# Where rows are transposed, normed and kept between the stages of a transformer block: a change to a one-core kernel

## The chip, the core and the metric

The kernel runs on one core of a Trainium2 chip. The core has a matrix engine (TensorE, "PE" in the profile, with its weight loads as "PEld"), a vector engine (VectorE, "DVE"), an activation engine (ScalarE, "ACT"), a general engine (GpSimd, "POOL") and a queue that issues most of the transfers (SyncE, "SP"). Each engine takes its instructions in the order in which the program lists them; engines wait for each other through semaphores. Data is worked on in an on-chip memory of 128 partitions (SBUF); products of PE land in eight accumulation banks (PSUM), from which DVE and ACT read. Transfers between DRAM and SBUF run on 16 DMA engines.

The metric is the time of one execution in microseconds (us) on the device.

## The reference

One transformer block on 1024 rows of 1024 features, in float32: a mixer of two sparse attentions, a cross-attention over 256 memory rows, and an MLP, each added to the residual stream. Only what the change touches is shown.

```python
def _memory_xattn(h, mem, mem_norm_g, w_xq, w_xk, w_xv, xq_norm_g, xk_norm_g, w_xo):
    m = _rms_norm(mem, mem_norm_g)
    q = _rms_norm((h @ w_xq).reshape(B, L, 4, 128), xq_norm_g)
    k = _rms_norm((m @ w_xk).reshape(B, M, 4, 128), xk_norm_g)
    v = (m @ w_xv).reshape(B, M, 4, 128)
    p = softmax(einsum('bqhd,bmhd->bhqm', q, k) * 128 ** -0.5)
    o = einsum('bhqm,bmhd->bqhd', p, v).reshape(B, L, 512)
    return o @ w_xo

def _sq_relu_mlp(h, w_ff_in, w_ff_out):
    return square(relu(h @ w_ff_in)) @ w_ff_out

x = x + _hybrid_mixer(_rms_norm(x, norm1_g), ...)      # ends in o @ w_out
x = x + _memory_xattn(_rms_norm(x, norm2_g), mem, ...)
x = x + _sq_relu_mlp(_rms_norm(x, norm3_g), w_ff_in, w_ff_out)   # 1024 -> 4096 -> 1024
```

## The kernel before

The 1024 rows are eight tiles of 128. PE needs its operands with the contracted dimension on the partitions, so rows are transposed on PE (a product with the identity `ident`) before a product uses them: `to_T` transposes up to four blocks of 128 columns into one PSUM buffer, and ACT and DVE copy the result out, either whole (one copy) or split in two parts `hi` and `lo` whose sum is the full value.

**Two streams.** The attention of the mixer (`attend`) runs over the eight tiles in order; it writes its outputs to DRAM (`oT_dr`, 64 KB pieces). Beside it runs a second stream, `fill`, which holds the rest: the projection of the later rows, `memory` (keys and values of the memory rows), then

- `between(dn, 0, 2, ...)` for tiles 0 and 1,
- `between(dn, 2, 2, ..., True)` for tiles 2 and 3,
- `mlp(dn, 0, 4, ...)`, the MLP of tiles 0 to 3,
- `between(dn, 4, 2, ...)` for tiles 4 and 5.

`together` draws from both streams by weights and paces; each `yield` hands over a weight. What attention leaves unfinished of `fill` runs after it, merged with `between(d2, 6, 2, ...)` for tiles 6 and 7, and `mlp_tail` closes with the MLP of tiles 4 to 7. On top of that order the framework orders the instructions of each engine by its own timeline before they are laid down; what is laid down is then fixed.

**`between`** does, for two tiles: load the attention output (`o_of`, eight pieces per tile, L927) and the input rows (`x2`, L931); the output product with `w_out` in four column chunks of 256, each added to `x2` (`add_to`, L918); norm and transpose (`norm_T2`); the query product with `w_xq` in two chunks; for each tile and chunk a `memory_item` (query norm, transposes, scores, softmax, transposes, values); the output product with `w_xo`, again added to `x2`.

`memory_item` writes its output `o` (128 rows by 256 columns) to DRAM at L1005 (`xo_dr`). After both chunks the rows are read back at L1011 and transposed four blocks at a time into `xh`, the buffer that had held the normed input of the query product. At the end the sums `x2` are kept in SBUF for tiles 2, 3, 6 and 7 (`keep`), and stored to DRAM (`x2_dr`, L1019) for tiles 0, 1, 4 and 5, to be loaded again by `mlp` (L1026) or `mlp_tail` (L1093).

**`norm_T2`** squares a tile with a row sum (ACT, L301), takes the inverse root (DVE L237, POOL L239), and for each half multiplies by it and by the gain (DVE, L305) and transposes (PE L282, ACT and DVE L243 and L244).

**`mlp`** norms its four tiles one after the other, then walks the 4096 features in eight groups: product with `w_ff_in`, square of the positive part, product with `w_ff_out`, added to the rows. Weights come in raw (`wraw`) and are split into `whi` and `wlo` (ACT L252, DVE or POOL L257). **`mlp_tail`** does the same for tiles 4 to 7: it loads the gain (L1086), norms tiles 4 and 5, runs two groups for them, then norms 6 and 7.

**Rings and pools.** A ring is a tag with a number of buffers; an allocation takes the one that came free first and waits until its last reader is through. In pool `dn` the tag `b4` (rows of one tile, 4 KB per partition) has four buffers. Pool `res` (tag `b4`, four buffers) lives from the end of attention to the end of the kernel; `d2` serves tiles 6 and 7; `d3`, the tail's pool, lies where `dn` was. In PSUM the tag `M` (psM) has one buffer, `D` (psD), `S` and `PT` have two.

Of the kernel before, what the change touches and what calls it, by code (L numbers as in the profile page):

```python
# [9 lines left out]
F32 = mybir.dt.float32  # L10
# [6 lines left out]
AF = mybir.ActivationFunctionType  # L17
ALU = mybir.AluOpType
# [4 lines left out]
P = 128  # L23
L = 1024
DM = 1024
# [13 lines left out]
    "p1": {"x4": 5, "st": 2, "relu": 4, "wraw": 4, "whi": 6, "wlo": 6, "c8": 4, "c4": 2, "kraw": 5, "pc": 2},  # L39
    "p2": {"x4": 5, "st": 1, "relu": 2, "whi": 4, "wlo": 4, "c8": 3, "c4": 1, "kraw": 4, "pc": 2},  # L40
    "dn": {"b4": 4, "h": 8, "relu": 2, "wraw": 2, "whi": 4, "wlo": 4},
    "res": {"b4": 4},
    "d2": {"b4": 2, "h": 8, "relu": 2, "whi": 4, "wlo": 4},
    "d3": {"g": 2, "h": 16, "relu": 2, "wraw": 4, "whi": 10, "wlo": 10},
}
PSUMS = {"p1": {"D": 4, "M": 3, "C": 1}, "main": {"S": 2, "PT": 2, "PV": 1, "D": 2, "M": 1}}
TAGS = {"p1": ("D", "M", "C"), "p2": ("D", "M", "D"), "dn": ("D", "M"), "d2": ("S", "PT"), "d3": ("D", "M")}
# [123 lines left out]
def build(nc, tc, I, C, out):  # L171
# [23 lines left out]
    def row(ap):  # L195
        return ap[None, :]
# [165 lines left out]
    KX = [[dr.tile([P, 2, 256], F32R, tag=f"KX{a}{c}", name=f"KX{a}{c}") for c in range(2)] for a in range(2)]  # L362
    VX = [[dr.tile([P, 2, 256], F32R, tag=f"VX{a}{c}", name=f"VX{a}{c}") for c in range(2)] for a in range(2)]
    x2_dr = [dr.tile([P, DM], F32, tag=f"x2{t}", name=f"x2{t}") for t in range(NT)]
    xo_dr = [dr.tile([P, 512], F32, tag=f"xo{t}", name=f"xo{t}") for t in range(NT)]


    ahead = {0: late["x"]}
# [545 lines left out]
    def residual_add(x2):  # L914
        def add_to(ci, t, pt):
            w = pt.shape[-1]
            dst = x2[t][:, ci * w:(ci + 1) * w]
            v.tensor_tensor(dst, pt, dst, op=ALU.add)  # L918
        return add_to

    def between(pool, t0, nt, x2s, keep, res=None):

        o_of = []
        for t in range(nt):
            o = ring(pool, "b4", [P, 8, P])
            for c in range(8):
                nc.sync.dma_start(o[:, c, :], oT_dr[t0 + t][c])  # L927
            o_of.append(o)
        x2 = [ring(res or pool, "b4", [P, DM]) for t in range(nt)]
        for t in range(nt):  # L930
            nc.sync.dma_start(x2[t], I["x"][0, (t0 + t) * P:(t0 + t + 1) * P, :])  # L931
        add_to = residual_add(x2)
        four = [[(c * 256, 256)] for c in range(4)]
        yield from gemm(pool, [lambda t, k: o_of[t][:, k, :]], 8, nt, W["w_out"], four, add_to)
        _, xf, xt_of = xT(pool, nt, True)

        gb2 = gain2(pool, W["norm2_g"])
        for t in range(nt):
            norm_T2(pool, x2[t], gb2, xt_of(t))
            yield 1.0  # L940

        kx, pts = [], {}

        def consume_q(ci, t, pt):
            if t == 0:
# [12 lines left out]
        def memory_item(ci, t, pt):  # L958

            (kh, kl), (vh, vl) = kx  # L960
            q = ring(pool, "relu", [P, 2, 2, P])
            p3 = pt.rearrange("p (h d) -> p h d", d=P)
            s.activation(q[:, 1], p3, AF.Square)
            ss = small(pool, "xss", 2)
            v.tensor_reduce(ss, q[:, 1], axis=AX.X, op=ALU.add)
            v.tensor_tensor(q[:, 0], p3, xqg[:, None, :].to_broadcast([P, 2, P]), op=ALU.mult)
            r = rsqrt_of(pool, ss, P, 2, "xq")
            sc = small(pool, "xsc", 4).rearrange("p (a h) -> p a h", a=2)
            v.tensor_scalar(sc[:, 0, :], r, XSCALE, None, op0=ALU.mult)
# [12 lines left out]
            v.tensor_tensor(nb, nb, sc[:, 1, :], op=ALU.mult)  # L982
            pr = ring(pool, "relu", [P, 2, 256])
            for h in range(2):
                s.activation(pr[:, h, :], sp[:, h, :], AF.Exp, bias=nb[:, h:h + 1],
                             scale=sc[:, 0, h:h + 1], accum_out=sums[:, h:h + 1])
            yield 1
            p2 = pst(TAGS[pool.name][1], [P, 2, 2, P])
            for k in range(2):
                for h in range(2):  # L990
                    te.transpose(p2[:, k, h, :], pr[:, h, k * P:(k + 1) * P], ident)
# [12 lines left out]
            v.tensor_tensor(o, pv, sums[:, :, None].to_broadcast([P, 2, P]), op=ALU.mult)  # L1004
            nc.sync.dma_start(xo_dr[t0 + t][:, ci * 256:(ci + 1) * 256], o.rearrange("p h d -> p (h d)"))  # L1005

        yield from gemm(pool, xf, 8, nt, W["w_xq"], [[(0, 256)], [(256, 256)]], consume_q)

        for t in range(nt):
            o = ring(pool, "relu", [P, 512])  # L1010
            nc.sync.dma_start(o, xo_dr[t0 + t])  # L1011
            to_T(pool, o, [x[:, 0:4] for x in xt_of(t)], 4)
            yield 0.5
        yield from gemm(pool, xf, 4, nt, W["w_xo"], four, add_to)
        for t in range(nt):
            if keep:
                x2s[t0 + t] = x2[t]
            else:
                nc.sync.dma_start(x2_dr[t0 + t], x2[t])  # L1019

    def mlp(pool, t0, nt, x2s):
        x2 = []
        for t in range(nt):
            if t0 + t not in x2s:
# [1 line left out]
                nc.sync.dma_start(x2s[t0 + t], x2_dr[t0 + t])  # L1026
            x2.append(x2s[t0 + t])
        add_to = residual_add(x2)
        (xh, xl), _, xt_of = xT(pool, nt)
        gb3 = gain2(pool, W["norm3_g"])  # L1030
        for t in range(nt):
            norm_T2(pool, x2[t], gb3, xt_of(t))
            yield 1.0

        for f4 in range(8):
# [41 lines left out]
                                          x2[t][:, c * 512:(c + 1) * 512])  # L1077
                    yield 2.6

    def mlp_tail(pool, res, x2s, t0):  # L1080

        x2 = {}
        (xh, xl), _, xt_of = xT(pool, 4)
        gb3 = [ring(pool, "g", [P, 512]) for _ in range(2)]
        for i, gb in enumerate(gb3):
            nc.sync.dma_start(gb, row(W["norm3_g"][i * 512:(i + 1) * 512]).to_broadcast([P, 512]))  # L1086

        def start(t):
            if t0 + t in x2s:
# [134 lines left out]
    dn_pool = tc.tile_pool(name="dn", bufs=1, reuse_waits="tile")  # L1224
    aw = aw_pool.__enter__()
    projected = []

    def fill():
        for part in range(1, len(PARTS)):
            with tc.tile_pool(name="p2", bufs=1, reuse_waits="tile") as p2:  # L1230
                yield from project(p2, part, late, st)
            projected.append(part)
        dn = dn_pool.__enter__()
        yield from memory(dn)
        yield 1, PACES[1]
        yield from between(dn, 0, 2, {}, False)
        yield 3, PACES[2]
        x2s = {}
        yield from between(dn, 2, 2, x2s, True)
        yield 3, PACES[3]  # L1240
        yield from mlp(dn, 0, 4, x2s)
        yield 5, PACES[4]
        yield from between(dn, 4, 2, {}, False)

    rest = fill()
    together(attend(aw, st), rest, projected)
# [1 line left out]
    sp_pool.__exit__(None, None, None)  # L1248
    at_pool.__exit__(None, None, None)
    res_pool = tc.tile_pool(name="res", bufs=1, side="right", reuse_waits="tile")  # L1250
    res = res_pool.__enter__()
    d2_pool = tc.tile_pool(name="d2", bufs=1, side="right", reuse_waits="tile")
    plan["w"] = PLAN_TAIL
    d2 = d2_pool.__enter__()
    x2s = {}
    rest = (w for w in rest if not isinstance(w, tuple))
    merge((rest, REST), (between(d2, 6, 2, x2s, True, res), 45.0))
    dn_pool.__exit__(None, None, None)
    d2_pool.__exit__(None, None, None)
    with tc.tile_pool(name="d3", bufs=1, reuse_waits="tile") as d3:  # L1260
        mlp_tail(d3, res, x2s, 4)
    res_pool.__exit__(None, None, None)
    ctx.close()

# [20 lines left out]
```

## Time and profile before

| | |
|---|---|
| median of 3 runs | 1806.75 us (1803.96 to 1807.26) |
| profiled execution: its time | 1806.83 us |
| profiled execution: span, first to last instruction | 1805.1 us |
| mean granted clock of PE | 0.979 of full speed |
| PE / DVE / ACT / POOL busy | 94% / 56% / 55% / 49% of the span |
| stores of `xo` (L1005) / reloads (L1011) | 16 of 128 KB / 8 of 256 KB |

The profile is of one execution. A row of the timeline has start, duration, engine, line, operation, out<-in by the program's names, shape and count, and in brackets the idle time of the engine just before it with what ended it. Names carry no buffer numbers. A product of float32 operands that are not split shows as two records. "PEclk" or the clock column is the clock that PE was granted. A group of lines has busy time, mean ns of one, and the idle time before with its releasers.

### The profile page before, as it was taken

How to read it: one execution, taken by the hardware profiler on the slowest of the kernel's cores; microseconds unless marked ns; L12 is line 12 of the kernel's file. 1: busy time of each engine (PE TensorE's matmuls, PEld its weight loads, DVE VectorE, ACT ScalarE, POOL GpSimd, SP SyncE). 2: the span in 40 equal slices, each digit the busy share in tenths (PEclk: the TensorE clock that was granted, in tenths of full speed). 3: DMA queues.
4: the chain of work that ended last, by engine and by line, in shares of the span. 5: the costliest groups of instructions: out<-in, count | busy, mean ns of one | idle time of the engine just before them, and what ended most of it. 6: DMA issues, size and time to landing. Idle time of an engine off the chain costs nothing.

```text
span 1805.1 us, 28037 instructions
## 1 busy us (share of the span) xinstructions
PE 1699.0 (94%) x9326; PEld 1458.2 (81%) x9326; DVE 1005.5 (56%) x2809; ACT 984.9 (55%) x2303; POOL 887.3 (49%) x1025
## 2 busy tenths in 40 slices
PE   7989999999989988999999999999999889999998
PEld 6987887788878877788878788788788778888887
DVE  4556779865885786656765667536234452222223
ACT  5444777853784688457955598555123443333333
POOL 2356557553541444575676666653111354444445
PEclk9999999899999999999999999999999899999999
DMA  7434221455336221222222121224774552333333
GB/s 199 118 129 113 64 64 58 164 161 167 97 111 188 85 61 36 60 68 71 64 75 64 63 72 60 63 70 135 229 227 124 182 155 88 95 95 96 97 120 107
DMA packets 176977, 193.80 MB, mean 107 GB/s; under 512 B 25664, under 2 KB 144192, under 8 KB 176832
## 3 DMA queue, kind: packets, MB, share of 16 engines
q1 hardware_dynamic: 168896, 181.52, 32.9%
q0 software_dynamic: 7936, 10.49, 2.1%
q8 instruction: 74, 1.21, 0.3%
q14 instruction: 71, 0.58, 0.1%
HBM read 170.98 MB, written 20.97 MB: 106 GB/s over the span
## 4 chain that ended last, share of the span: by engine, by line
PE 53%; DVE 7%; ACT 5%; issue 3%; DMA 2%; POOL 1%; SPq 0%; DVEq 0%; POOLq 0%; ACTq 0%
PE psD L224 39%; PE psS L224 7%; PE psPV L224 3%; PE psPT L721 2%; ACT dmask L662 2%; DMA relu<-xo 1%; DVE tkj L663 1%; ACT whi L252 1%; DMA whi<-in_w_out_dram 1%; PE psM L282 1%; ACT S L706 1%; ACT ph L243 1%; DVE pl L244 1%; DVE S L704 0%; POOL wlo L257 0%
## 5 line engine op out<-in xcount | busy, mean ns | idle before, releaser
L257 POOL TENSOR_TENSOR wlo<-wraw,whi 128x512 fp32r<-128x512 f32 (+1 forms) x225 | 307.8, 1373 | 272.4 <-ACT whi L252 269.6
L224 PE MATMUL psD<-whi,h 128*128 128x512 f32 x1024 | 338.4, 399 | 9.7 <-DVE b L1150 7.1
L252 ACT ACTIVATE whi<-wraw 128x512 fp32r<-128x512 f32 x321 | 200.3, 627 | 220.6 <-PE psD L224 158.4
L224 PEld LDWEIGHTS psD<-whi,h 128*128 128x128 f32 x1024 | 191.7, 189 | 53.5 <-DVE b L1150 10.9
L224 PE MATMUL psD<-xh,whi 128*128 128x512 f32 (+1 forms) x576 | 212.8, 373 | 1.6 <-ACT xh L243 1.5
L224 PE MATMUL psD<-xh,wlo 128*128 128x512 f32 (+1 forms) x576 | 213.1, 371 | 0.0
L224 PE MATMUL psD<-xl,whi 128*128 128x512 f32 (+1 forms) x576 | 211.2, 369 | 0.0
L224 PE MATMUL psD<-wlo,h 128*128 128x512 f32 x512 | 201.6, 396 | 0.3 <-POOL wlo L257 0.3
L224 PE MATMUL psD<-wlo,xh 128*128 128x256 f32 (+1 forms) x704 | 192.5, 355 | 2.9 <-DMA wlo<-in_w_in_dram 2.4
L224 PE MATMUL psD<-whi,xh 128*128 128x256 f32 (+1 forms) x704 | 191.3, 353 | 1.5 <-DVE Vd L244 0.9
L244 DVE TENSOR_TENSOR pl<-psPT,ph 128x512 fp32r<-128x512 f32 (+1 forms) x232 | 141.7, 619 | 58.9 <-ACT ph L243 58.0
L706 ACT ACTIVATE S<-S,mn 128x128 f32<-128x128 f32 (+7 forms) x192 | 142.9, 745 | 50.4 <-DVE mn L704 49.3
L243 ACT ACTIVATE ph<-psPT 128x512 fp32r<-128x512 f32 (+1 forms) x232 | 122.1, 540 | 86.2 <-PE psPT L721 76.6
L257 DVE TENSOR_TENSOR wlo<-wraw,whi 128x512 fp32r<-128x512 f32 (+1 forms) x96 | 81.5, 849 | 149.6 <-ACT whi L252 149.6
L711 POOL TENSOR_SCALAR S<-S,sums,gi 128x640 f32<-128x640 f32 (+7 forms) x128 | 105.3, 832 | 100.2 <-DVE sums L709 95.2
L224 PEld LDWEIGHTS psD<-wlo,xh 128*128 128x128 f32 x704 | 132.9, 194 | 14.1 <-DMA wlo<-in_w_in_dram 2.8
L224 PEld LDWEIGHTS psD<-whi,xh 128*128 128x128 f32 x704 | 131.3, 194 | 11.6 <-DVE Vd L244 1.1
L721 PE MATMUL psPT<-c_ident,S 128*128 128x128 f32 x816 | 133.9, 278 | 7.0 <-POOL S L711 2.1
L224 PEld LDWEIGHTS psD<-xh,whi 128*128 128x128 f32 x576 | 108.5, 188 | 19.1 <-ACT xh L243 2.0
L224 PEld LDWEIGHTS psD<-xl,whi 128*128 128x128 f32 x576 | 108.6, 189 | 17.6
L224 PEld LDWEIGHTS psD<-xh,wlo 128*128 128x128 f32 x576 | 108.5, 188 | 17.0
L224 PE MATMUL psS<-K,qh 128*128 128x384 f32 (+3 forms) x288 | 111.7, 392 | 9.9 <-DVE mn L704 6.1
(289 smaller groups left out, 3830.2 us busy)
## 6 DMA issues: line engine op xcount, KB each, us to landing
wraw<-in_w_ff_in_dram SPq DMA_DIRECT2D x40, 512.0 KB, 4.0
wraw<-in_w_ff_out_dram SPq DMA_DIRECT2D x40, 512.0 KB, 3.9
wraw<-in_w_ff_in_dram SPq DMA_DIRECT2D x64, 256.0 KB, 2.8
wraw<-in_w_ff_out_dram SPq DMA_DIRECT2D x64, 256.0 KB, 2.7
whi<-in_w_out_dram SPq DMA_DIRECT2D x32, 256.0 KB, 4.2
wlo<-in_w_out_dram SPq DMA_DIRECT2D x32, 256.0 KB, 4.1
wraw<-in_w_in_dram SPq DMA_DIRECT2D x24, 256.0 KB, 3.7
q<-st SPq DMA_DIRECT2D x12, 512.0 KB, 2.8
```

The lines of the kernel that those rows point to most:

```text
L224: te.matmul(o, a, b, start=start, stop=stop)
L243: s.activation(hi, src, AF.Copy)
L244: v.tensor_tensor(lo, src, hi, op=ALU.subtract)
L252: s.activation(hi, raw, AF.Copy)
L257: (v if l == "v" else g).tensor_tensor(lo, raw, hi, op=ALU.subtract)
L282: te.transpose(pt[:, j, :], x_t[:, (c + j) * P:(c + j + 1) * P], ident)
L662: s.activation(mask, src, AF.Sign, bias=tks[:, i, 1:2], accum_out=over[:, 0:1])
L663: v.scalar_tensor_tensor(small(aw, "tkj", 3), over, nd, tks[:, i, :], op0=ALU.is_gt, op1=ALU.mult, accum_out=tks[:, i + 1, 1:2] if b else ...
L706: s.activation(S, S, AF.Exp, bias=low, scale=-1.0, accum_out=sums[:, hh:hh + 1])
L711: g.tensor_scalar(Ss[hh], Ss[hh], sums[:, hh:hh + 1], 1.0 if gate is None else gate[:, hh:hh + 1], op0=ALU.mult, op1=ALU.mult)
L721: te.transpose(p2[:, j, hh, :], S[:, (c + j) * P:(c + j + 1) * P], ident)
```

## The change

Three things move, and two rings change with them.

1. `memory_item` no longer stores `o`. It transposes it at once (two blocks) into `xo`, a fifth row tile of tag `b4`; `xo_dr`, the stores and the reloads are gone, and the product with `w_xo` reads `xo`.
2. For tiles 2 and 3, `between` alternates its product with `w_xo` with `pre_norms`, which norms tiles 0 and 1 for the MLP: tile 0 is loaded whole, tile 1 in two halves into `wraw`. `mlp` then norms tiles 2 and 3 alone. The rows of tile 1 are loaded a second time for the residual sum.
3. For tiles 4 and 5, once `res` is open, the sums are written to tiles of `res` (`kept`) by the last add and handed to `mlp_tail` in `x2s`; they are neither stored nor loaded. The gain `gb3` moves from `d3` to `res` and is loaded as soon as `res` is open.

```diff
-    "res": {"b4": 4},
+    "res": {"b4": 4, "g": 2},
-    "d3": {"g": 2, "h": 16, "relu": 2, "wraw": 4, "whi": 10, "wlo": 10},
+    "d3": {"h": 16, "relu": 2, "wraw": 4, "whi": 10, "wlo": 10},
...
-    def between(pool, t0, nt, x2s, keep, res=None):
+    def between(pool, t0, nt, x2s, keep, res=None, then=None):
...
         kx, pts = [], {}
+        xo = ring(pool, "b4", [P, 4, nt * P])
...
             v.tensor_tensor(o, pv, sums[:, :, None].to_broadcast([P, 2, P]), op=ALU.mult)
-            nc.sync.dma_start(xo_dr[t0 + t][:, ci * 256:(ci + 1) * 256], o.rearrange("p h d -> p (h d)"))
+            yield 1
+            to_T(pool, o.rearrange("p h d -> p (h d)"), [xo[:, ci * 2:ci * 2 + 2, t * P:(t + 1) * P]], 2)
...
-        for t in range(nt):
-            o = ring(pool, "relu", [P, 512])
-            nc.sync.dma_start(o, xo_dr[t0 + t])
-            to_T(pool, o, [x[:, 0:4] for x in xt_of(t)], 4)
-            yield 0.5
-        yield from gemm(pool, xf, 4, nt, W["w_xo"], four, add_to)
+        if not keep and "res" in late:
+            kept = [ring(late["res"], "b4", [P, DM]) for t in range(nt)]
+            x2s.update((t0 + t, kept[t]) for t in range(nt))
+
+            def add_to(ci, t, pt):
+                cs = slice(ci * 256, (ci + 1) * 256)
+                v.tensor_tensor(kept[t][:, cs], pt, x2[t][:, cs], op=ALU.add)
+        last = gemm(pool, [lambda t, k: xo[:, k, t * P:(t + 1) * P]], 4, nt, W["w_xo"], four, add_to)
+        yield from alternate(last, then()) if then else last
         for t in range(nt):
             if keep:
                 x2s[t0 + t] = x2[t]
-            else:
+            elif t0 + t not in x2s:
                 nc.sync.dma_start(x2_dr[t0 + t], x2[t])
 
+    def pre_norms(pool, made, x2s):
+
+        made["x"] = xT(pool, 4)
+        made["g"] = gain2(pool, W["norm3_g"])
+        xt_of = made["x"][2]
+        x2s[0] = ring(pool, "b4", [P, DM])
+        nc.sync.dma_start(x2s[0], x2_dr[0])
+        norm_T2(pool, x2s[0], made["g"], xt_of(0))
+        yield 1.0
+        halves_ = []
+        for c in range(2):
+            halves_.append(ring(pool, "wraw", [P, 512]))
+            nc.sync.dma_start(halves_[c], x2_dr[1][:, c * 512:(c + 1) * 512])
+        xs = xt_of(1)
+        ss = [small(pool, "nss", 1) for _ in range(2)]
+        for c in range(2):
+            s.activation(xs[0][:, c * 4:c * 4 + 4], halves_[c].rearrange("p (k c) -> p k c", c=P), AF.Square, accum_out=ss[c])
+        v.tensor_tensor(ss[0], ss[0], ss[1], op=ALU.add)
+        r = rsqrt_of(pool, ss[0], DM, 1, "n")
+        yield 0.5
+        for c in range(2):
+            xn = ring(pool, "relu", [P, 512])
+            v.scalar_tensor_tensor(xn, halves_[c], r[:, 0:1], made["g"][c], op0=ALU.mult, op1=ALU.mult)
+            to_T(pool, xn, [x[:, c * 4:c * 4 + 4] for x in xs], 4)
+            yield 0.5
+
-    def mlp(pool, t0, nt, x2s):
+    def mlp(pool, t0, nt, x2s, made):
...
-        (xh, xl), _, xt_of = xT(pool, nt)
-        gb3 = gain2(pool, W["norm3_g"])
-        for t in range(nt):
-            norm_T2(pool, x2[t], gb3, xt_of(t))
+        (xh, xl), _, xt_of = made["x"]
+        for t in range(2, nt):
+            norm_T2(pool, x2[t], made["g"], xt_of(t))
             yield 1.0
...
-    def mlp_tail(pool, res, x2s, t0):
+    def mlp_tail(pool, res, x2s, t0, gb3):
...
-        gb3 = [ring(pool, "g", [P, 512]) for _ in range(2)]
-        for i, gb in enumerate(gb3):
-            nc.sync.dma_start(gb, row(W["norm3_g"][i * 512:(i + 1) * 512]).to_broadcast([P, 512]))
...
-        x2s = {}
-        yield from between(dn, 2, 2, x2s, True)
+        x2s, made = {}, {}
+        yield from between(dn, 2, 2, x2s, True, None, lambda: pre_norms(dn, made, x2s))
...
-        yield from between(dn, 4, 2, {}, False)
+        yield from between(dn, 4, 2, late["x2s"], False)
...
-    res = res_pool.__enter__()
+    res = late["res"] = res_pool.__enter__()
+    gb3 = [ring(res, "g", [P, 512]) for _ in range(2)]
+    for i, gb in enumerate(gb3):
+        nc.sync.dma_start(gb, row(W["norm3_g"][i * 512:(i + 1) * 512]).to_broadcast([P, 512]))
...
-    x2s = {}
+    x2s = late["x2s"]
...
-        mlp_tail(d3, res, x2s, 4)
+        mlp_tail(d3, res, x2s, 4, gb3)
```

More of the change, by code (lines that the diff above doesn't have):

```diff
@@ L364, in build @@
     x2_dr = [dr.tile([P, DM], F32, tag=f"x2{t}", name=f"x2{t}") for t in range(NT)]
-    xo_dr = [dr.tile([P, 512], F32, tag=f"xo{t}", name=f"xo{t}") for t in range(NT)]
     ahead = {0: late["x"]}
@@ L931, in between @@
             nc.sync.dma_start(x2[t], I["x"][0, (t0 + t) * P:(t0 + t + 1) * P, :])
-        add_to = residual_add(x2)
-        four = [[(c * 256, 256)] for c in range(4)]
+        add_to, four = residual_add(x2), [[(c * 256, 256)] for c in range(4)]
         yield from gemm(pool, [lambda t, k: o_of[t][:, k, :]], 8, nt, W["w_out"], four, add_to)
@@ L1226, in build @@
     projected = []
+    late["x2s"] = {}
     def fill():
@@ L1237, in fill @@
         yield 3, PACES[2]
-        x2s = {}
-        yield from between(dn, 2, 2, x2s, True)
+        x2s, made = {}, {}
+        yield from between(dn, 2, 2, x2s, True, None, lambda: pre_norms(dn, made, x2s))
         yield 3, PACES[3]
-        yield from mlp(dn, 0, 4, x2s)
+        yield from mlp(dn, 0, 4, x2s, made)
         yield 5, PACES[4]
-        yield from between(dn, 4, 2, {}, False)
+        yield from between(dn, 4, 2, late["x2s"], False)
     rest = fill()
```

## The prediction

> **What bounds the kernel now.** I read the page first, then the granted clock, then where TensorE (PE) stands still.
>
> ```profile
> span 1805.1 us, 28037 instructions
> PE 1699.0 (94%) x9326; PEld 1458.2 (81%) x9326; DVE 1005.5 (56%) x2809; ACT 984.9 (55%) x2303; POOL 887.3 (49%) x1025
> ...
> PE 53%; DVE 7%; ACT 5%; issue 3%; DMA 2%; POOL 1%; SPq 0%; DVEq 0%; POOLq 0%; ACTq 0%
> ```
>
> PE sets the pace: it is busy for 94% of the span and no other engine for more than 56%. The change alters no product of the big weights, so it can gain only from the 1805.1 - 1699.0 = 106.1 us in which PE is idle and from time at a halved clock. The second view cuts out the two stages that the change rearranges: the attention over the memory of tiles 2 and 3 with the start of the MLP after it (641 to 730), and the same change of stage in the tail (1382 to 1442). Its columns are busy us of the engines, granted clock, DMA share and GB/s.
>
> ```profile
> 641.00:670.00 29.00, 27.21 (x165) 24.22 (x165) 22.45 (x83) 26.53 (x59) 13.27 (x15) 1.00 0.20 56
> 670.00:699.50 29.50, 20.97 (x115) 17.25 (x116) 27.49 (x80) 25.32 (x57) 14.38 (x19) 0.88 0.06 17
> ...
> 1382.00:1397.00 15.00, 14.36 (x76) 12.47 (x74) 5.79 (x18) 2.84 (x9) 0.69 (x1) 1.00 0.35 110
> 1397.00:1401.00 4.00, 2.80 (x19) 2.25 (x19) 1.97 (x4) 2.54 (x7) 0.00 (x0) 0.98 0.82 277
> 1401.00:1418.00 17.00, 9.13 (x33) 7.26 (x34) 10.41 (x14) 7.65 (x16) 6.25 (x6) 0.50 0.83 256
> 1418.00:1442.00 24.00, 24.00 (x159) 22.49 (x158) 6.92 (x14) 9.22 (x19) 9.51 (x12) 1.00 0.41 132
> ...
> 1134.60:1138.00 3.40, 3.40 (x11) 2.63 (x10) 3.40 (x7) 2.23 (x5) 3.32 (x3) 0.50 0.27 83
> 1264.30:1267.70 3.40, 3.40 (x9) 2.69 (x10) 0.00 (x0) 0.00 (x0) 0.96 (x2) 0.50 1.13 375
> ```
>
> From 670 to 699.5 VectorE (DVE) is full (27.49 of 29.5) and ScalarE (ACT) nearly, because four norms run there beside attention and no big product is at hand; PE idles 8.5 us, and the mean clock of 0.88 means some 7 us at 0.5, another 3.5 us lost. From 1397 to 1418 PE idles 1.2 + 7.9 us, and its 9.13 busy us at clock 0.50 are worth 4.6, so 13.6 us are lost there. PE's own rows, with the idle time before each in brackets, show who is waited for:
>
> ```profile
> 1393.15 1.03 PE L224 MATMUL psD<-whi,xh 128*128 128x256 f32 x4
> 1394.02 1.03 PE L224 MATMUL psD<-wlo,xh 128*128 128x256 f32 x4
> ...
> 1397.77 1.33 PE L224 MATMUL psS<-h 128*128 128x128 f32 x10
> 1398.94 0.51 PE L991 MATMUL psPT<-c_ident,relu 128*128 128x128 f32 x3
> ...
> 1405.98 1.11 PE L282 MATMUL psM<-c_ident,relu 128*128 128x128 f32 x4 [2.66 <-DVE relu L305]
> 1408.57 1.11 PE L282 MATMUL psM<-c_ident,relu 128*128 128x128 f32 x4 [1.47 <-DVE xl L244]
> 1410.79 1.12 PE L282 MATMUL psPT<-c_ident,relu 128*128 128x128 f32 x4 [1.11 <-DMA relu<-xo]
> 1414.53 1.09 PE L282 MATMUL psM<-c_ident,relu 128*128 128x128 f32 x4 [2.62 <-DVE xl L244]
> ...
> 1418.20 0.47 PE L224 MATMUL psD<-xh,whi 128*128 128x256 f32 x1
> ```
>
> The last output product of tiles 4 and 5 ends near 1394.9 and the first MLP product starts at 1418.2, 23.3 us later. The queues say why: first SP's issues, then one row each of DVE, ACT and GpSimd (POOL).
>
> ```profile
> 1392.88 0.34 SPq L1019 DMA_DIRECT2D x<-b  x1
> 1395.56 0.34 SPq L1093 DMA_DIRECT2D b<-x  x1
> ...
> 1399.97 0.92 SPq L1086 DMA_DIRECT2D g<-in_norm_g_dram  x2
> ...
> 1401.41 1.00 SPq L1104 DMA_DIRECT2D wraw<-in_w_ff_in_dram  x2
> ```
> ```profile
> 1405.18 0.75 DVE L305 SCALAR_TENSOR_TENSOR relu<-b,nr,g 128x512 f32<-128x512 f32 x1 [3.80 <-DMA g<-in_norm_g_dram]
> ```
> ```profile
> 1408.72 1.14 ACT L252 ACTIVATE whi<-wraw 128x512 fp32r<-128x512 f32 x2
> ```
> ```profile
> 1409.94 3.30 POOL L257 TENSOR_TENSOR wlo<-wraw,whi 128x512 fp32r<-128x512 f32 x2 [0.29 <-ACT whi L252]
> ```
>
> The sums of tile 4 go out to DRAM and come back, the gain vector is asked for only at 1399.97, and the first weights of the MLP stand behind both in SP's queue.
>
> **The change, part by part.** The order of the built instructions, compared engine by engine, tells where each part went.
>
> **Sums of 4 and 5 to the tail's room.** Two stores (x<-b) and two reloads (b<-x) go, and the gain is loaded far ahead. In the new order the transposes of norms 4 and 5 stand among the queries of tiles 6 and 7, and between the last output product of 4 and 5 and the first MLP product stand 15 query products, 18 transposes and 12 narrow products. A 256-column product takes 0.43 us (two rows, 1393.15 to 1394.02, are 0.87 apart for two products of two records each), a transpose 0.15 to 0.17, a narrow one 0.13: 6.5 + 2.9 + 1.6 = 11.0 us of work. The weights could be there sooner: their buffers come free with that last output product, and from issue to the first split were at most 1408.72 - 1401.41 = 7.3 us, plus 0.6 (ACT) and 1.65 (POOL) for the split, 9.6 us. So the wait for weights is covered, with 1.4 us to spare; if the cover is gone it costs what is over. The item chains of tiles 6 and 7 (softmax between products) now have MLP products to hide behind. What is late next is the odd softmax link (0.7 us before) and perhaps one stretch at half clock: 3.6 us left of 13.6, gain 10. Bounds: 4 (only the waits on the gain and the stores, 2.66 + 1.11, go) and 13.6.
>
> The clock term rests on idle time driving the clock, as the rows at 1134.6 and 1264.3 suggest: 3.4 us at 0.50 each. [...]
>
> **Norms of 0 and 1 beside the product of 2 and 3.** What one norm costs, from the groups of lines between 641 and 700:
>
> ```profile
> L305 DVE SCALAR_TENSOR_TENSOR relu<-b,nr,h 128x512 f32<-128x512 f32 x8 | 6.4, 806 | 1.2 <-POOL nr L239 0.7 <-PE psM L282 0.5
> ...
> L244 DVE TENSOR_TENSOR xl<-psM,xh 128x512 fp32r<-128x512 f32 x7 | 4.7, 678 | 0.3 <-ACT xh L243 0.3
> ...
> L301 ACT ACTIVATE xh<-b 128x1024 fp32r<-128x1024 f32 x4 | 4.2, 1048 | 0.0
> L243 ACT ACTIVATE xh<-psM 128x512 fp32r<-128x512 f32 x7 | 4.1, 590 | 0.4 <-PE psM L282 0.3
> ```
>
> DVE 2 x 0.806 + 2 x 0.678 = 3.0 us, ACT 1.05 + 2 x 0.59 = 2.2 us. Two norms take 6.0 us of DVE out of the stretch where DVE is the limit, which shortens it by about that, and some 1.7 us of half clock go with it. They land in 641 to 670, where DVE has 6.5 us free but ACT only 2.5 for 4.4: 1.9 us are paid there. The new order has 80 PE rows without a big product where there were 139, the rest now lies beside MLP products. Net 6.0 + 1.7 - 1.9 = 5.8; because waits in the crowded stretch can come at the wrong time I take 4. Bounds: a loss of 2 (nothing freed, ACT paid) and a gain of 9 (three quarters of 12). The two half loads of tile 1 and the gain's place in the queue add three SP issues of about 0.35 us in a stage where DMA is busy for 0.20; they are hidden by attention.
>
> **Memory rows transposed at once.** Sixteen stores and eight reloads go, and with them PE's waits on the reload outside the tail stretch. The new short transposes (two instead of four at a time) share the one buffer psM with the norms:
>
> ```profile
> PE psM L282 <- DVE xl L244: 11.2, 5, 3.8
> PE psD L224 <- DVE b L918: 3.6, 3, 2.2
> PE psM L282 <- DMA relu<-xo: 3.2, 3, 1.7
> ```
>
> The gain is 3.2. In the new order 13 or more PE rows stand between an item's value products and its transposes, so they rarely wait; I charge 1.2 and keep 2. Bounds: 0 and 3.2. **The ring** pays: five row tiles go through four buffers (tag b4). The loads of tile 3's attention output must wait until the output product of 0 and 1 has ended, and the input rows of 2 and 3 queue behind them on SP, with output weights behind those. Before:
>
> ```profile
> x<-b SPq DMA_DIRECT2D x4, 512.0 KB, 4.1
> b<-o SPq DMA_DIRECT2D x64, 64.0 KB, 2.1
> b<-in_x_dram SPq DMA_DIRECT2D x8, 512.0 KB, 4.3
> ```
>
> Nine issues of 0.46 us (the row at 1399.97 has two in 0.92) and a landing of 2.1 put tile 3 there 6.2 us after that product; the input rows of tile 2 land at 4.1 + 4.3 = 8.4, and the add that frees a product buffer takes another 0.4. PE has one tile's product (eight at 0.43, 3.5 us), ten attention instructions (at 0.17, 1.7) and the second tile's product (3.5) to do meanwhile, 8.7 us. So it is a tie, where PE now waits 2.2 us (second row of the waits above, its longest); I charge 1 more, and 5 if the store, too, is slow.
>
> **Sum.** -10 - 4 - 2 + 1 = -15 on the profiled execution: span 1805.1, its time 1806.8, so 1.7 us lie around it. 1790.1 + 1.7 = 1791.8, say **1792 us**. That execution lies 0.1 above the median of 1806.75, so nothing is corrected. All gains at their best and no loss give 1806.8 - 25.8 = 1781; all at their worst 1806.8 - 4 + 2 + 5 = 1810.
>
> **Rivals.** (1) The weights of the first MLP products are late all the same. For it: four 512 KB blocks start at once, DMA is at 0.83 there, and four loads for the product of 6 and 7 stand ahead of them on SP. Against: 7.3 us was measured in that very crowd. If the distance of 23.3 us stays, 12.3 are left over the 11.0 of cover, and PE, which goes in order, holds the items of 6 and 7 back with it; the tail gains 1.3: 1800.5. (2) The half clock does not follow from these gaps and stays: 4.6 + 1.7 us come back, 1798. Against it: clock and idle time fall together in every row above. [...] (3) Slower: the single psM buffer. Twelve short rounds and four rounds of norms 0 and 1 now come between products that PE takes in order; a waited-for round cost 11.2 / 5 = 2.2 us. At seven such waits the 15 us are gone, with ten it is 1806.8 - 15 + 22 = 1814. For it: ACT and DVE, which empty psM, are full between 641 and 700. Against it: those 11.2 us are five waits in the whole run, mostly where PE had nothing else. (4) The stall only moves: the items' own softmax chains become what PE waits for in the tail, and the crowded ACT undoes the gain at 670; tail -3, the rest 0: 1804. That the sums of 4 and 5 still pass through DRAM is no rival: the stores x<-b fall from 4 to 2 in the built order.
>
> **How the numbers follow.** Forecast 1786 to 1798: 0.52; more than that, below 1786: 0.09; rival 1: 0.13; rival 2: 0.06; rival 4: 0.09; rival 3: 0.11. What a measurement of this kernel can tell from no change is about 0.2%, 3.6 us, so faster means below 1803.1: 0.52 + 0.09 + 0.13 + 0.06 = 0.80; same, up to 1810.4: 0.09; slower 0.11. The range is 1781 to 1805: it leaves out rival 3 and half of what may lie below.
>
> **What would show it.** After: no relu<-xo among PE's waits; no stretch of ten and more us at clock 0.50 near 1400; the first xh,whi product within some 12 us of the last output product of 4 and 5; PE above 25 of 29.5 us in the stretch before the MLP's first product; the L918 wait before the second output product of 2 and 3 between 1 and 7 us. The forecast is wrong if psM L282 rises above 20 us among PE's waits, if wraw is what PE or ACT waits for in the tail, or if the half clock lasts with the idle time gone.

## The result, and the profile after

Four runs of the changed kernel have a median of 1793.9 us (1789.2 to 1796.5), four of the kernel before beside them 1806.9 us (1804.0 to 1807.3). The ratio is 0.9929, 95% interval 0.9905 to 0.9952: faster by 0.7%, near the 1792 us of the prediction. The profiled execution took 1789.2 us. Its first lines, in the form of the page of before:

```profile
span 1787.5 us, 27978 instructions
PE 1688.9 (94%) x9326; PEld 1452.9 (81%) x9326; DVE 1008.9 (56%) x2810; ACT 984.9 (55%) x2313; POOL 891.2 (50%) x1025
```

PE's idle time is 1787.5 - 1688.9 = 98.6 us, where it was 106.1, and its busy time is 10.1 us shorter with the same 9326 records, most of it time at half clock: the mean clock is 0.984, where it was 0.979. So the gain of this pair of profiles is made of waits and clock; 5.7 us of it lie ahead of the first point that the change touches, as the last section says. The same stretches as in the prediction, in the view by windows (busy us of PE, PEld, DVE, ACT and POOL, granted clock, DMA share, GB/s): the 29.3 us before the MLP's first product, then the tail, and a stretch that was not expected to matter, 1295.6 to 1302.4.

```profile
648.00:677.30 29.30, 24.86 (x142) 22.08 (x141) 24.32 (x79) 27.85 (x64) 16.53 (x21) 0.88 0.24 75
1376.00:1387.80 11.80, 7.94 (x41) 6.62 (x39) 8.05 (x14) 7.32 (x15) 7.05 (x7) 1.00 0.93 303
1387.80:1394.60 6.80, 4.54 (x19) 3.91 (x20) 6.27 (x14) 2.02 (x4) 2.66 (x3) 0.50 0.68 245
...
1295.60:1302.40 6.80, 3.42 (x8) 2.76 (x9) 0.00 (x0) 0.00 (x0) 1.69 (x4) 0.50 1.01 305
```

Before the MLP, DVE fell from 27.5 to 24.3 us and PE rose from 21.0 to 24.9; ACT is the fuller engine there now (27.85 us), and the clock is 0.88 as before. In the tail, 1376.0 to 1394.6 loses 3.9 + 2.3 us of idle time and 2.3 at half clock, 8.4 in all, where 13.6 were lost: a gain of 5.2. The last line takes it back. PE's rows with the waits in both places, first the one of before, then those of after:

```profile
1304.09 0.45 PE L224 MATMUL psS<-whi,b 128*128 128x256 f32 x1 [1.79 <-DMA whi<-in_w_out_dram]
```
```profile
1298.98 0.80 PE L224 MATMUL psS<-whi,b 128*128 128x256 f32 x1 [4.95 <-DMA whi<-in_w_out_dram]
...
1375.70 0.38 PE L224 MATMUL psD<-wlo,b 128*128 128x256 f32 x1
...
1385.58 0.50 PE L224 MATMUL psS<-h 128*128 128x256 f32 x2 [2.15 <-ACT h L243]
1389.44 0.69 PE L282 MATMUL psPT<-c_ident,relu 128*128 128x128 f32 x2 [3.36 <-DVE relu L965]
...
1395.64 0.39 PE L224 MATMUL psD<-xh,whi 128*128 128x256 f32 x1 [0.75 <-ACT xh L243]
```

The output product of tiles 6 and 7 waited 1.79 us for its weights before; now it waits 4.95, and the clock halves around it (3.42 busy us there are worth 1.7). That is 3.2 + 1.7 = 4.9 us lost against 5.2 won. The second profile of the changed kernel (after_again below) agrees: there the wait is 6.77 us, and of the 19.6 us from the last output product of 4 and 5 to the MLP's first product 6.7 are idle, here 6.9. In the tail it is no longer weights, gain or sums that PE waits for, but the items of tiles 6 and 7 themselves. SP's rows of before, and then of after, show where the 4.95 us come from, and two lines of what SP itself waited for among the pieces of after:

```profile
1290.34 0.59 SPq L735 DMA_DIRECT2D o<-oc  x1
1290.98 6.78 SPq L927 DMA_DIRECT2D b<-o  x14
1297.86 0.85 SPq L931 DMA_DIRECT2D b<-in_x_dram  x2
1298.75 0.43 SPq L273 DMA_DIRECT2D whi<-in_w_out_dram  x1
```
```profile
1281.43 0.93 SPq L1280 DMA_DIRECT2D g<-in_norm_g_dram  x2
1282.45 0.59 SPq L734 DMA_DIRECT2D o<-oc  x1
1283.09 1.07 SPq L930 DMA_DIRECT2D b<-in_x_dram  x2
...
1284.73 10.40 SPq L926 DMA_DIRECT2D b<-o  x16
1295.23 0.38 SPq L273 DMA_DIRECT2D whi<-in_w_out_dram  x1
```
```profile
SPq L926 <- DMA b<-in_x_dram: 1.6, 2, 1.0
SPq L926 <- DMA g<-in_norm_g_dram: 1.0, 2, 0.8
```

From the store of attention's last output (o<-oc) to the issue of the first output weight it was 8.4 us and is now 12.8. Gain and input rows are issued ahead of the pieces of the attention output, all sixteen pieces stand behind the store, where it was fourteen, and they take 10.4 us instead of 6.8. The pieces are not dearer to issue one by one (median 0.43 us in both): between them SP stands still until the rows and the gain that it has just issued have landed, 2.6 us in all. Before, SP had no such wait among its pieces.

### The profile page after: what moved, and what is told of

Read it like the earlier page. It is cut to its first block, busy times and chain, and to the rows that moved or that the text cites. A ratio compares the mean times of both kernels' runs of the same rounds, so it can differ in the third digit from the quotient of the medians.

```text
span 1787.5 us, 27978 instructions
## 1 busy us (share of the span) xinstructions
PE 1688.9 (94%) x9326; PEld 1452.9 (81%) x9326; DVE 1008.9 (56%) x2810; ACT 984.9 (55%) x2313; POOL 891.2 (50%) x1025
## 4 chain that ended last, share of the span: by engine, by line
PE 65%; DVE 10%; ACT 9%; DMA 5%; POOL 5%; issue 4%; SPq 1%; ACTq 0%; POOLq 0%; DVEq 0%
PE psD L224 48%; PE psS L224 8%; ACT dmask L661 4%; PE psPV L224 3%; PE psPT L720 3%; ACT S L705 2%; POOL wlo L257 1%; DVE pl L244 1%; DVE S L703 1%; PE psM L282 1%; DVE tkj L662 1%; ACT whi L252 1%; DMA wraw<-in_w_ff_in_dram 1%; ACT ph L243 1%; POOL S L710 1%
## 5 line engine op out<-in xcount | busy, mean ns | idle before, releaser
L224 PE MATMUL psD<-whi,h 128*128 128x512 f32 x1024 | 343.7, 402 | 9.4 <-DVE b L1175 5.4
L224 PE MATMUL psD<-wlo,xh 128*128 128x256 f32 (+1 forms) x608 | 165.7, 348 | 2.8 <-DMA wlo<-in_w_in_dram 2.4
L224 PE MATMUL psD<-whi,xh 128*128 128x256 f32 (+1 forms) x608 | 165.9, 347 | 1.3 <-DVE Vd L244 0.9
L224 PEld LDWEIGHTS psD<-wlo,xh 128*128 128x128 f32 x608 | 113.6, 193 | 11.4 <-DMA wlo<-in_w_in_dram 2.8
L224 PEld LDWEIGHTS psD<-whi,xh 128*128 128x128 f32 x608 | 112.9, 193 | 9.4 <-DVE Vd L244 1.1
```

Of the source, the lines that this page charges most:

```text
L224: te.matmul(o, a, b, start=start, stop=stop)
```

## The experiments

Each kernel was timed in five rounds against the kernel before on the same chip; as the times of before differ from chip to chip (medians 1807 to 1814 us), the ratio is what is compared. PE's idle time is span less busy time of the profiled execution, the clock is of that execution.

| kernel | ratio to before, 95% | PE idle us | clock |
|---|---|---|---|
| before | 1 | 106.1 | 0.979 |
| the change | 0.9929 (0.9905 to 0.9952) | 98.6 | 0.984 |
| after_again: the change once more | 0.9932 (0.9911 to 0.9953) | 104.0 | 0.980 |
| a_once: transposes at once alone | 0.9888 (0.9869 to 0.9908) | 99.5 | 0.983 |
| b_kept: sums kept, gain early, alone | 1.0012 (0.9993 to 1.0031) | 107.2 | 0.976 |
| e_norms: norms of 0 and 1 alone | 0.9973 (0.9955 to 0.9991) | 106.2 | 0.978 |
| c_no_norms: a_once and b_kept | 0.9906 (0.9887 to 0.9924) | 99.8 | 0.981 |
| a_head: at once, tiles 0 to 3 only | 0.9877 (0.9850 to 0.9905) | 94.0 | 0.980 |
| a_tail: at once, tiles 4 to 7 only | 0.9948 (0.9929 to 0.9968) | 103.4 | 0.985 |
| x_head_paced: a_head, yields left in | 0.9926 (0.9904 to 0.9949) | 98.8 | 0.979 |
| x_before_unpaced: before, yields out | 0.9933 (0.9910 to 0.9957) | 99.8 | 0.982 |
| g_late: c_no_norms, gain moved | 0.9875 (0.9851 to 0.9898) | 95.7 | 0.986 |
| x_after_late: the change, gain moved | 0.9910 (0.9886 to 0.9934) | 104.6 | 0.981 |
| g_late_split: g_late, two queues | 0.9837 (0.9813 to 0.9861) | 94.1 | 0.982 |

**The parts one by one.** On the kernel before, first the transposes alone:

```diff
-            nc.sync.dma_start(xo_dr[t0 + t][:, ci * 256:(ci + 1) * 256], o.rearrange("p h d -> p (h d)"))
+            yield 1
+            to_T(pool, o.rearrange("p h d -> p (h d)"), [xo[:, ci * 2:ci * 2 + 2, t * P:(t + 1) * P]], 2)
...
-        for t in range(nt):
-            o = ring(pool, "relu", [P, 512])
-            nc.sync.dma_start(o, xo_dr[t0 + t])
-            to_T(pool, o, [x[:, 0:4] for x in xt_of(t)], 4)
-            yield 0.5
```

> The kernel before with the memory rows transposed at once alone (fifth row tile in the ring of four buffers, no stores and reloads of xo; norms and sums as before). Theory P, the terms of the prediction: -2 for the waits on the reload, +1 for the ring, so 1806 (-1 against before). Theory S, that the gain sits in the stages and not in the terms as I cut them: on record after the change, the stretch from the last output product of 4 and 5 to the first MLP product of the tail shrank by 3.6 us only, and the transposes now stand among the queries of 6 and 7; by it most of the tail's gain comes from not waiting for the reload relu<-xo, which holds PE's order, and this part alone brings 4 to 7 us: 1800 to 1803. Either way no relu<-xo among PE's waits; the wait on the gain (relu<-b,nr,g) stays in the tail.

Measured 0.9888, some 20 us: three times the larger of the two forecasts, and more than the whole change. The wait on the gain nearly went too, from 3.3 to 1.0 us (psM L282 <- DVE relu L305), against both expectations. The edit also takes out two `yield 0.5` per call, which matters below.

The kept sums alone are the change's third part put on the kernel before: `kept`, `x2s` handed on, `gb3` in `res`.

> The kernel before with the sums of 4 and 5 kept in res and the gain loaded early, alone (xo still through DRAM, norms of 0 to 3 in the MLP). Theory P: -10, so 1797. Theory S: the items of 6 and 7 and their reload of xo are what PE then waits for between the last output product of 4 and 5 and the MLP: -3 to -6, so 1801 to 1804. Both: no wait on g in the tail; by P no stretch of ten and more us at clock 0.50 near the start of the tail, by S one of about 7 or more stays.

Measured 1.0012: nothing, or a small loss. PE's rows of that kernel and the windows of two stretches at half clock:

```profile
1311.69 0.79 PE L224 MATMUL psS<-whi,b 128*128 128x256 f32 x1 [6.13 <-DMA whi<-in_w_out_dram]
...
1408.87 0.66 PE L282 MATMUL psM<-c_ident,relu 128*128 128x128 f32 x4 [2.10 <-DVE relu L305]
1415.14 2.39 PE L224 MATMUL psS<-h 128*128 128x128 f32 x10 [1.38 <-DVE h L244]
```
```profile
1410.20:1423.90 13.70, 9.91 (x45) 9.16 (x44) 10.63 (x15) 7.56 (x15) 8.04 (x5) 0.50 0.62 194
1307.80:1314.60 6.80, 2.91 (x7) 2.38 (x8) 0.00 (x0) 0.00 (x0) 0.00 (x0) 0.50 1.07 333
```

The tail still loses 3.8 us of idle time and 5.0 at half clock in 1410.2 to 1423.9, with no gain and no sums to wait for: norms and items hold PE. And the weights of 6 and 7 come late here too, 6.13 us, which with the half clock behind that wait (2.91 busy us are worth 1.5) costs 4.3 + 1.5 us and takes back what the tail wins, 13.6 - 8.8.

The norms alone are `pre_norms` beside the w_xo product of 2 and 3.

> The kernel before with the norms of tiles 0 and 1 beside the w_xo product of 2 and 3, alone. Theory P: -4, so 1803. Theory S, by the place of the MLP's end in the trace after the change (14.7 us earlier, of which 5.7 were there before the change could act): -7 to -9, so 1798 to 1800. Both: DVE below 27 of 29.5 us in the stretch before the MLP's first product.

Measured 0.9973, 5 us: the prediction's 4 was right for this part by itself. Then the changed kernel without `pre_norms`, that is, the first and third part together:

> The changed kernel with the norms of tiles 0 and 1 back in the MLP (the two other parts stay). Theory P: -11, so 1796. Theory S: -4 to -7, so 1800 to 1803, since most of the gain is the norms'. If the parts add up, this time and that of the norms alone have differences from before that sum to that of the whole change, -13.

Measured 0.9906, some 17 us, more than either forecast. The parts don't add up: 0.9888, 1.0012 and 0.9973 multiplied give 0.9873, the whole gives 0.9929. Whether that was chance was asked with the changed kernel, unaltered:

> The changed kernel, unaltered, once more, to set it beside the parts on one chip. Theory Q (the transposes at once bring the whole gain; the two other parts give some of it back): ratio to before 0.992 to 0.994 as in the first measurement, so 4 to 9 us slower than the transposes alone (ratio 0.9888). Rival (the first measurement and that of the parts differ by chip or by luck): ratio 0.988 to 0.990, as the transposes alone.

0.9932. Its interval and that of the transposes alone, taken on two chips, don't touch (that of the first measurement, from 0.9905, just does): **the transposes bring more than the whole change, and the two other parts together give back some 0.4%.**

**Where the transposes gain.** `once = t0 < 4`, or `t0 >= 4`, chooses between the new path and the old per call of `between`.

> Transposed at once for tiles 0 to 3 only; tiles 4 to 7 go through DRAM as before, norms and sums as before. By the trace of the kernel with the transposes alone, the stages from the first output product of 2 and 3 to the end of the MLP of 0 to 3 are 12.7 us shorter, of which about 4 are attention work put off to later, and the rest up to the norms of 6 and 7 is 3.9 us shorter with these 4 in it. Theory Q1 (both places gain): about -8 here, ratio 0.995 to 0.9965. Rival Q2 (the tail gains nothing by itself, what is seen there comes from attention having moved): -14 to -18, ratio 0.990 to 0.992. Rival Q3 (all gain in the tail): ratio above 0.998.

> Transposed at once for tiles 4 to 7 only; tiles 0 to 3 through DRAM as before. Q1: about -8, ratio 0.995 to 0.9965, with no relu<-xo wait after 1300 us and the first tail product of the MLP earlier by 8 or more. Q2: ratio above 0.998. Q3: 0.989 to 0.991.

0.9877 and 0.9948: each place gains by itself, but the first alone already gives what both give. No theory said so. Built, the kernel with the tail's transposes has PE in the same order as before until 1344 us, so its 9 us are of the tail alone. (Its two calls lose their yields too, and the streams of the tail are merged by the same weights; how much of the 9 us is the reload and how much the order was not tried apart.) The windows from the psD<-h wait near 485 us to the MLP's first product, through the MLP of 0 to 3, and on to the norms of 6 and 7: all three of before, the last one of tail only, then all three of head only.

```profile
485.06:699.20 214.14, 193.68 (x1150) 168.33 (x1150) 161.61 (x538) 151.66 (x364) 80.31 (x113) 0.98 0.35 104
699.20:1253.04 553.84, 540.35 (x2806) 451.44 (x2807) 336.42 (x861) 356.03 (x714) 355.44 (x350) 0.99 0.22 68
1253.04:1476.67 223.63, 201.87 (x1129) 177.08 (x1128) 90.56 (x195) 74.88 (x160) 58.82 (x69) 0.95 0.62 191
```
```profile
1255.28:1468.75 213.47, 197.57 (x1129) 173.34 (x1128) 92.16 (x195) 75.18 (x164) 60.14 (x69) 0.99 0.60 190
```
```profile
481.81:692.95 211.14, 196.28 (x1150) 171.66 (x1150) 157.64 (x533) 151.31 (x366) 79.38 (x112) 0.94 0.32 98
692.95:1240.75 547.80, 536.22 (x2781) 449.14 (x2780) 335.17 (x853) 353.05 (x709) 355.03 (x349) 0.99 0.21 69
1240.75:1459.09 218.34, 202.79 (x1156) 179.60 (x1154) 93.96 (x209) 78.01 (x169) 61.45 (x71) 0.97 0.62 195
```

With the tail's transposes alone the last stretch is 10.2 us shorter with the same 1129 PE records: 5.9 us less idle, the rest clock (0.95 to 0.99). The MLP's first product of the tail is not earlier for it, though that was foretold (1420.96, before 1418.20); instead 110 PE records stand between it and the last output product of 4 and 5, where 64 stood. With the head's alone it is 5.3 us shorter although it holds 27 records more and its memory rows still pass through DRAM: idle time falls there from 21.8 to 15.6 us by another order alone. The MLP's 6.0 us are 4.1 of busy time, most of it attention work put off to the last stretch, and 1.9 of idle time. Ahead of the MLP idle time falls from 20.5 to 14.9 us, of which the clock of that execution (0.94) takes some back.

**Order or reload?** Those two `yield 0.5` per call count, since `together` weighs its two streams by what they yield (`df += w or 0.0`). So that was tried apart for tiles 0 to 3: the yields left in, and, in the kernel before, set to nothing for tiles 0 to 3 with the reloads left.

```diff
+            for t in range(nt):
+                yield 0.5
```

> The kernel with the transposes at once for tiles 0 to 3 only (ratio 0.9877), but with the two yields of 0.5 per call left in that stood behind the reloads; they count as work in the weights by which the second stream and attention take turns, so taking them out let the second stream run 1.0 ahead per call, and from PE's 3400th product on the instructions are interleaved otherwise. Theory reload (stores, reloads and their place in PE's order are what costs): ratio stays at 0.986 to 0.990. Rival pace (the gain is a better interleave of the MLP of 0 to 3 with attention that the two yields decide): ratio 0.995 to 1.000, of which at most 3 us are the reload's.

```diff
-            yield 0.5
+            yield 0.5 if t0 >= 4 else 0.0
```

> The kernel before, with stores and reloads of the memory rows, and the two yields of 0.5 behind the reloads of tiles 0 to 3 set to 0. Theory reload: ratio 0.998 to 1.002. Rival pace: ratio 0.988 to 0.992.

0.9926 and 0.9933: both theories fall as put, each has half. Without touching one transfer, four yields of 0.5 (two in each of two calls) are worth 0.7%; with them kept, the reloads of tiles 0 to 3, with the new places of the transposes, are worth 0.7%. With the yields kept the stretch up to the MLP's first product is 6.2 us shorter than before and its idle time falls from 20.5 to 15.1 us:

```profile
484.21:692.20 207.99, 192.88 (x1150) 168.63 (x1150) 157.42 (x533) 150.88 (x364) 79.38 (x112) 0.97 0.33 100
```

The MLP's stretch in the kernel before with the yields out, and what PE waits for between 700 and 1240 us, first of before, then of this kernel:

```profile
698.76:1244.80 546.04, 538.42 (x2793) 451.11 (x2794) 335.57 (x855) 354.09 (x711) 354.53 (x348) 0.99 0.22 69
```
```profile
PE psS L224 <- DVE mn L704: 4.5, 3, 2.1
PE psS L224 <- ACT ir L628: 3.5, 2, 2.4
...
PE psPT L721 <- DVE sums L709: 1.4, 1, 1.4
```
```profile
PE psS L224 <- ACT ir L628: 5.1, 3, 3.0
...
PE psS L224 <- DVE mn L704: 0.2, 1, 0.2
```

Idle time there falls from 13.5 us (553.84 - 540.35) to 7.6. Two waits on attention's own chain (mn, sums) are all but gone, 5.9 us before; the one on ir grows by 1.6.

**The weights of tiles 6 and 7.** The load of the gain was moved in the code behind the output product of 6 and 7, in the kernel without the early norms and in the changed one:

```diff
+        if res:
+            for i, gb in enumerate(late["gb3"]):
+                nc.sync.dma_start(gb, row(W["norm3_g"][i * 512:(i + 1) * 512]).to_broadcast([P, 512]))
         _, xf, xt_of = xT(pool, nt, True)
```

> Transposes at once and sums of 4 and 5 kept, norms of 0 and 1 back in the MLP, and the gain of the tail's norms loaded only behind the output weights of 6 and 7, not as soon as its room opens. Beside it stands the same kernel with the gain loaded first (ratio 0.9906; PE waits 7.7 us for w_out of tiles 6 and 7 there, 1.9 with the transposes alone). Theory Q (gain and rows taken ahead on SP push the pieces of the attention output and the weights back): the wait on w_out of 6 and 7 falls to 2 to 4 us and the ratio to 0.986 to 0.988. Rival R (the room's new layout delays the pieces, whatever the gain's place): the wait stays at 5 to 8 us and the ratio at 0.990 to 0.992.

> The changed kernel with one thing other: the gain of the tail's norms is loaded behind the output weights of 6 and 7. Theory Q (in the kernel without the early norms this step took the wait on w_out of 6 and 7 from 7.7 to 2.6 us and the ratio from 0.9906 to 0.9875): wait from 5 to 7 down to 2 to 3 us, ratio 0.989 to 0.991, 4 to 6 us below the changed kernel. Rival: the gain is only late elsewhere (a wait on g in the norms of 4 and 5 of 2 us and more), ratio 0.992 to 0.994.

PE's rows: without the early norms and with the gain first (c_no_norms), then with the gain moved (g_late), then the changed kernel with it moved; behind each of the last two, SP's rows.

```profile
1307.35 1.22 PE L224 MATMUL psS<-whi,b 128*128 128x256 f32 x2 [7.68 <-DMA whi<-in_w_out_dram]
```
```profile
1301.16 0.80 PE L224 MATMUL psS<-whi,b 128*128 128x256 f32 x1 [2.63 <-DMA whi<-in_w_out_dram]
...
1284.53 0.90 SPq L936 DMA_DIRECT2D g<-in_norm_g_dram  x2
1285.53 0.85 SPq L734 DMA_DIRECT2D o<-oc  x1
...
1297.45 0.38 SPq L273 DMA_DIRECT2D whi<-in_w_out_dram  x1
```
```profile
1310.22 0.80 PE L224 MATMUL psS<-whi,b 128*128 128x256 f32 x1 [7.49 <-DMA whi<-in_w_out_dram]
...
1290.75 2.04 SPq L935 DMA_DIRECT2D g<-in_norm_g_dram  x2
...
1302.69 1.14 SPq L273 DMA_DIRECT2D whi<-in_w_out_dram  x1
```

The edit didn't do what I meant. The planner put the gain ahead of the pieces all the same, only behind the input rows (in the changed kernel behind the store as well), so the time from the last store to the first output weight hardly changed (11.9 and 13.3 us, after 13.9 in c_no_norms and 12.8 in the change). In g_late the wait fell and so did the ratio, though the intervals 0.9875 and 0.9906 overlap by a hair; in the changed kernel the wait stayed and the ratio of 0.9910 can't be told from 0.9932. A gain that really comes behind the pieces was not tried. What holds is the comparison of kernels: where sums and gain sit in `res`, the wait is 4.95 and 6.77 (the change, twice), 6.13, 7.68, 7.49 and, in g_late, 2.63 us; before it is 1.79, with the transposes alone 1.87, with the norms alone 3.39.

Last, SP's burden itself: g_late with every other piece of tiles 6 and 7 on POOL's queue.

```diff
-                nc.sync.dma_start(o[:, c, :], oT_dr[t0 + t][c])
+                (g if res and c % 2 else nc.sync).dma_start(o[:, c, :], oT_dr[t0 + t][c])
```

> Transposes at once, sums kept, gain late (ratio 0.9875), and every other piece of the attention output of tiles 6 and 7 issued on POOL's queue instead of SP's. If SP's sixteen issues in a row (0.4 to 0.65 us each) are what the output weights of 6 and 7 wait for, the wait falls from 2.6 to under 1 us and the time by 2 to 3 us: ratio 0.985 to 0.987. Rival: the pieces are late for another reason (POOL's own work delays its issues, or the landing rules): ratio 0.987 to 0.990.

```profile
1288.60 0.59 SPq L734 DMA_DIRECT2D o<-oc  x1
...
1296.12 0.38 SPq L273 DMA_DIRECT2D whi<-in_w_out_dram  x1
...
1299.79 0.48 PE L224 MATMUL psS<-whi,b 128*128 128x256 f32 x1 [1.37 <-DMA whi<-in_w_out_dram]
```

From store to weight it is 7.5 us again, the wait 1.37 (not under 1), and 0.9837 the best ratio of all, 1.6% below the kernel before and below the range foretold. Against g_late, measured on another occasion, the intervals overlap (0.9851 to 0.9861), so how much of it is the second queue's stays open.

## Why the prediction was right, and where it was not

The time was right (1792 against 1793.9 us), and the sign. The sum behind it was not: its terms were -10, -4, -2 and +1, and two of them, measured alone, lie outside their bounds. That they cancelled is luck.

- **Sums kept, -10.** Bounds -4 to -13.6; alone it measures +2 us (-1 to +6). The step that failed is the attribution of the tail's 13.6 us: I read the waits on gain and sums and SP's order as their cause, and charged the cure to the sums alone. The same edit put gain and rows ahead of sixteen pieces on SP and made PE wait 4 us longer for w_out of 6 and 7, a wait that the sum doesn't have: I counted what comes sooner and not what stands behind it on the same queue. In the changed kernel the account is 5.2 won and 4.9 lost.
- **Weights covered.** Right: no wait on wraw in the tail. But the MLP's first product came 19.6 us after the last output product (1395.64 - 1376.08), not within 12, since PE waits 2.15 + 3.36 us for the items and works 4.5 us at half clock. That is rival 4's mechanism in the tail; it had a chance of 0.09, with 3 us left of the tail's gain.
- **Transposed at once, -2.** Bounds 0 and 3.2; alone it measures some -20. The step that failed is the price: the waits that name relu<-xo. Transposing at once in the tail is worth 9 us there, yields included, by idle time and clock in a stretch whose rows name other waits. In the head it is worth 13 us with the yields kept, of which 6.2 show up to the MLP's first product (214.14 to 207.99): twice the 3.2 of the named waits in that stretch alone. The other half of the 22 with the yields out is those yields, which the diff shows and I didn't price: they change how the MLP of 0 to 3 and attention alternate.
- **The ring, +1.** It cost nothing that shows: before the second output product of 2 and 3, the waits below stand in after where 2.15 us (on b, L918) stood, and the first is just within the 1 to 7 foretold.

```profile
546.93 1.13 PE L224 MATMUL psD<-whi,b 128*128 128x256 f32 x4 [1.27 <-DVE b L917]
550.73 1.13 PE L224 MATMUL psD<-wlo,b 128*128 128x256 f32 x4 [0.94 <-DMA wlo<-in_w_out_dram]
```

- **Norms, -4.** Alone -5. On top of the two other parts the ratio goes from 0.9906 to 0.9929 and 0.9932, so no gain is left and perhaps a loss; the intervals overlap. PE in the stretch before the MLP is at 24.86 of 29.3, just short of the 25 foretold, but the 1.7 us of half clock that were to go there stayed (0.88). With the MLP starting 16 us earlier (22 by the profiles, less the 5.7 won ahead of the change), its own stage became longer; which order costs there was not settled. The part also yields 2.5 in `between` where `mlp` yielded 2.0, ahead of the change of pace, and no run parts this from the norms themselves.
- **Half clock.** The 17 us stretch is gone with part of the idle time; 6.8 us remain in the first profile. In the second profile of the same kernel 10.2 us remain, from 1399.2 on, and the forecast's "no stretch of ten and more" fails there. So rival 2 holds in part: of its 4.6 us 2.3 remain in the first profile, and the 1.7 before the MLP stayed. That idle time drives the clock, by which both terms went into the sum, was my estimate from rows of before; no run shows it by itself, as the last section says. Rival 3, the single psM buffer, is out: psM's waits on xl fell from 11.2 to 5.1 us among PE's waits:

```profile
PE psM L282 <- DVE xl L244: 5.1, 3, 3.8
```

## What to carry to other kernels

A right total proves nothing of its terms: run each part alone, since here one part alone beat the whole by 0.4%. In a kernel whose order is laid by a planner, look for what an edit does to the weights that it counts: four yields of 0.5, with no instruction changed, moved the time as much as taking out the eight stores and four reloads of the head. And the loads taken ahead were paid for here by what stood behind them on their queue: from the store to the first output weight 8.4 us became 12.8, in 2.6 of which the queue stood still until those loads had landed. So find the next thing for which an engine waits there before you call it free, and see in the built queue that the load went where the code says.

## What the runs showed of the hardware

The half clock came in pieces of 3.4 us (3.40, 6.80, 13.70 in the windows above), and the same wait did not always bring it. In the 17 us at 0.50 of the kernel before, from 1401 on, PE's longest wait is 2.66 us. In the two rows from which the prediction ties the clock to idle time, 1134.6 and 1264.3, PE is busy for all of the 3.40 us; the 3.4 us ahead of them, at clock 1.00, hold 1.95 and 1.89 us of its idle time. So idle time stands ahead of the half clock there and not in the same row. PE's wait for K near 312 us, of 2.17 us, in the profiles of before and of after, whose instructions have the same order up to some 479 us, and the window behind each:

```profile
313.77 0.66 PE L495 MATMUL psM<-c_ident,x 128*128 128x128 f32 x4 [2.17 <-DVE K L498]
...
315.40:318.80 3.40, 3.40 (x13) 3.14 (x12) 2.71 (x9) 3.38 (x13) 0.64 (x2) 0.50 0.22 63
```
```profile
310.31 0.66 PE L494 MATMUL psM<-c_ident,x 128*128 128x128 f32 x4 [2.17 <-DVE K L497]
...
311.90:315.30 3.40, 3.40 (x23) 3.14 (x21) 3.34 (x15) 3.12 (x10) 0.88 (x3) 1.00 0.21 60
```

The same instructions in the same place were halved in one execution and not in the other: 13 records against 23 in 3.4 us. In the second profile of the changed kernel, the very same program, the clock behind the same 2.17 us is 0.50 again (317.2 to 320.6). What decides it was not shown.

So one profile carries luck. The changed kernel's two profiled executions reached the first wait on psD<-h at 479.37 and 486.79 us, a point ahead of everything that the change touches, with mean clocks of 0.984 and 0.980 over the whole execution; 51 runs of the kernel before, beside the experiments, spread from 1803.2 to 1822.2 us with clocks from 0.982 down to 0.971. The pair of profiles in this document shows 17.6 us of gain, 5.7 of them ahead of the change (485.06 to 479.37), the runs 13.
